# The first feed-forward product of a two-layer hybrid backbone, computed per weight tile from seven half-sized products

## The chip, the core and the metric

The kernel runs on one core of one Trainium2 chip. Its engines are TensorE (PE, with PEld for the loads of its stationary operand), VectorE (DVE), ScalarE (ACT), GpSimd (POOL) and SyncE (SP); SP issues most transfers, POOL and ACT a few. The metric is the time of one execution on the device in microseconds; the median of three runs of the kernel before is 3309.47 us (3304.61 to 3312.08).

## What is computed

A generator's backbone of two layers runs over 1024 latent tokens and 256 context tokens of width 1024. Each layer normalises and modulates, mixes tokens with three groups of heads, and ends with a gated feed-forward stage (SwiGLU) of inner width 2816. The last layer drops the context after its keys and values.

```python
def swiglu(h, w_in, w_out):
    gate, up = jnp.split(h @ w_in, 2, axis=-1)
    return (jax.nn.silu(gate) * up) @ w_out

def hybrid_layer(xl, xc, sc, scc, ...):
    mod_l = sc @ w_mod + b_mod
    sh1, sc1, gt1, sh2, sc2, gt2 = [m[:, None, :] for m in jnp.split(mod_l, 6, axis=-1)]
    ...
    h2 = modulate(rms_norm(xl, g_ffn), sh2, sc2)
    xl = xl + gt2 * swiglu(h2, w_ffn_in, w_ffn_out)
```

(The last two lines are the reference's feed-forward stage in short.) The context goes through the same stage in layer one with modulations of its own.

## The kernel before, in words

Activations lie with channels on the 128 partitions and tokens along the free dimension, in eight tiles k of 128 channels. The latent tokens are two halves b of 512; the context is one group of 256. Every operand of a large product is split in two (`split`, L126 to L129): ACT rounds it to fp32r (L128), DVE subtracts to get the remainder (L129). A product is then three matmuls, high by high, low by high and high by low (`mm3`, L144 to L146). `weight` (L130 on) loads a weight tile on SP's queue (L135) into one of two buffers `wr` and splits it into `wh` and `wl`, two buffers each.

The feed-forward stage is `ffn` (L1051). It goes through 22 inner tiles f in blocks of 3, 3, 3, 3, 3, 3, 2, 2. For each f it loads the gate's and the up's weight tile (1024 columns wide after the split, eight k of 128) and computes for each token group 24 matmuls for the gate and 24 for the up into the two halves of one PSUM tile `ps_f`. ACT takes the Silu of the gate (L1074), DVE multiplies by the up (L1075), and the result is split into `gh` and `gl`, which stay in SBUF. At a block's end the second product adds the block's tiles to the residual stream: per output tile m, three matmuls per f and group into `ps_fo`, and DVE adds them to x (`residual`, L1002). The groups in layer one are half 0, context, half 1; in layer two there is no context. In the last block the groups are taken one after the other, each with its first and second product, and after each the next norm (layer one) or the final norm and the output (layer two) is done.

Ahead of the stage, `out_proj` computes half 1's last attention projection (L1194) while half 0 is normalised (L1190), and half 1 is normalised after it (L1196). The pages of this stage live in a pool that `phase` (L72) opens after the release of the attention's pool; x is loaded into it from DRAM (L1188). During layer one's stage, POOL computes the modulation sums of layer two (`mods_part`, L270 to L285): per 512 columns and k it loads 128 rows of `w_mod`, multiplies by the conditioning value of the row (L281) and adds (L283); `mods_sum` (L287) folds the sums on DVE.

No order is written out by hand. Each engine, SP's queue included, runs its instructions in a fixed order. The framework has set that order ahead of the run: an instruction is placed when its operands and its buffer are expected to be free, and among those that are free at once the one that stands earlier in the program goes first. PSUM has four kinds of buffers: two tiles `ps_s` of two banks, two tiles `ps_t`, one `ps_g` and one `ps_o`.

Of the kernel before, what the change touches and what calls it, by code (L numbers as in the profile page):

```python
# [9 lines left out]
F32 = mybir.dt.float32  # L10
# [5 lines left out]
T = 1024  # L16
# [37 lines left out]
class Net:  # L54
# [16 lines left out]

    def tl(self, shape=(128, 512), name="tl"):  # L72
        return self.pool.tile(list(shape), F32, tag="tl", name=name, bufs=4)
# [67 lines left out]
    def mm3(self, ps, w, x, first, last):  # L141
        (wh, wl), (xh, xl) = w, x
        mm = self.nc.tensor.matmul
        mm(ps, wh, xh, start=first, stop=False)  # L144
        mm(ps, wh, xl, start=False, stop=False)  # L145
        mm(ps, wl, xh, start=False, stop=last)  # L146


    def setup(self):
# [36 lines left out]
        self.tabd = [tc.dram_tile([4, 128, 896], F32, name=f"tabd{l}") for l in range(2)]  # L186
        self.yc_c = tc.dram_tile([128, 4, TC], F32, name="yc_c")
# [82 lines left out]
    def mods_part(self, l, c, pages):  # L270


        nc, G = self.nc, self.nc.gpsimd
        nj = 2 if l == 0 or c < 4 else 1
        acc = pages[:2]
        for k in range(KD):
            w, o = pages[2 + k % 2], pages[3 - k % 2]
            G.dma_start(w, self.a["w_mod"][l, k * 128:(k + 1) * 128, c * 512:(c + 1) * 512])
            for j in range(nj):
                to = acc[j] if k == 0 else o if j < nj - 1 else w  # L280
                G.tensor_tensor(to, w, self.sc[:, k, j:j + 1].to_broadcast([128, 512]), op=ALU.mult)  # L281
                if k > 0:
                    G.tensor_tensor(acc[j], acc[j], to, op=ALU.add)  # L283
        for j in range(nj):
            G.dma_start(self.modd[l][j, :, c * 512:(c + 1) * 512], acc[j])  # L285
# [765 lines left out]
    def ffn(self, l, groups, blocks, parts, done, aside=None, keep=False):  # L1051
# [4 lines left out]
        for bi, nf in enumerate(blocks):  # L1056
# [4 lines left out]

            for gi in [[i for i, _ in p] for p in parts] if last else [range(len(groups))]:
                gs = []
                for f in range(f0, f0 + nf):
                    wg, wu = self.wk(a["w_ffn_in"][l, f]), self.wk(a["w_ffn_in"][l, KF + f])
                    row = {}
                    for i in gi:
                        h, xs, n, j, place = groups[i]
                        gh, gl = place(f - f0)
                        ps = self.ps_s("ps_f")  # L1070
                        for p, w in enumerate((wg, wu)):
                            self.proj(ps[:, p * 512:p * 512 + n], w, h)
                        sg = self.hp(name="sg")[:, :n]
                        nc.scalar.activation(sg, ps[:, :n], AF.Silu)  # L1074
                        nc.vector.tensor_tensor(sg, sg, ps[:, 512:512 + n], op=ALU.mult)  # L1075
                        self.split(gh, gl, sg)
                        row[i] = (gh, gl)
                    gs.append(row)
                    if aside and gi[0] == 0:
                        aside(f)  # L1080
                pieces = dict(x for p in parts for x in p)
                for gj, c in [((i,), c) for i in gi for c in pieces[i]] if last else [(gi, None)]:
                    for m in range(KD):
# [6 lines left out]
                        for i in gj:  # L1090
                            h, xs, n, j, place = groups[i]
                            s = c or slice(0, n)
                            ps = self.ps_gt("ps_fo")[:, :s.stop - s.start]
                            for k in range(nf):
                                gh, gl = gs[k][i]
                                self.mm3(ps, (w[0][:, k], w[1][:, k]), (gh[:, s], gl[:, s]), k == 0, k == nf - 1)
                            self.residual(xs[m][:, s], ps, self.ls[l]["mod"][:, 40 + m, j:j + 1])
                    if last:
                        done(gj[0], c)
            f0 += nf  # L1100


    def run(self):
        nc, a, tc = self.nc, self.a, self.tc
        with ExitStack() as es:
# [29 lines left out]
            for l in range(2):  # L1135
# [50 lines left out]
                for b in range(2):  # L1186
                    for k in range(KD):
                        nc.sync.dma_start(xg[b][k], xd[:, k, tb[b]])  # L1188
                h2 = [(self.big("h2h"), self.big("h2l"))]
                self.norm(xg[0], 512, l, 1, 0, *h2[0], self.nw, self.ps_t)  # L1190
                if full:
                    h2c = (self.bigc("h2ch"), self.bigc("h2cl"))
                    self.norm(XC, TC, 0, 1, 1, *h2c, self.nw, self.ps_t)
                self.out_proj(l, 0, [(mix[1], xg[1], 512, 0, None, None)], self.ps_h, engine=nc.gpsimd)  # L1194
                h2.append((self.big("h2h"), self.big("h2l")))
                self.norm(xg[1], 512, l, 1, 0, *h2[1], self.nw, self.ps_t)  # L1196

                def place(b):
                    def p(f):
                        if b == 0:  # L1200
                            place.cur[f] = (self.pg(dt=F32R, name="gh"), self.pg(dt=F32R, name="gl"))
                        return tuple(t[:, tb[b]] for t in place.cur[f])
                    return p

                place.cur = {}
                turn = count()

                def placec(f):
                    t = self.pool.tile([128, 2, TC], F32R, tag="nw", name="gc", bufs=self.nnw)
                    return t[:, 0], t[:, 1]  # L1210
# [146 lines left out]
```

## Time and profile before

| | |
|---|---|
| median of three runs | 3309.47 us |
| the profiled execution, its time | 3303.53 us |
| the profiled execution, its span | 3301.7 us |
| TensorE busy | 3176.8 us, 96% |
| VectorE busy | 1704.9 us, 52% |
| ScalarE busy | 979.0 us, 30% |
| GpSimd busy | 542.2 us, 16% |
| layer one's feed-forward stage | about 880 to 1812 us |
| layer two's feed-forward stage | about 2549 us to the end |

Span means from the first to the last instruction. Views by stretch say how much of a stretch each engine was busy, with the clock that TensorE was granted as a share of full speed. The views by line group equal instructions; the timelines list single instructions with their start and duration, in brackets the idle time ahead of them and what ended it.

### The profile page before, as it was taken

How to read it: one execution, taken by the hardware profiler on the slowest of the kernel's cores; microseconds unless marked ns; L12 is line 12 of the kernel's file. 1: busy time of each engine (PE TensorE's matmuls, PEld its weight loads, DVE VectorE, ACT ScalarE, POOL GpSimd, SP SyncE). 2: the span in 40 equal slices, each digit the busy share in tenths (PEclk: the TensorE clock that was granted, in tenths of full speed). 3: DMA queues.
4: the chain of work that ended last, by engine and by line, in shares of the span. 5: the costliest groups of instructions: out<-in, count | busy, mean ns of one | idle time of the engine just before them, and what ended most of it. 6: DMA issues, size and time to landing. Idle time of an engine off the chain costs nothing. (4 is left out here: it accounts for less than half of the span.)

```text
span 3301.7 us, 41939 instructions
## 1 busy us (share of the span) xinstructions
PE 3176.8 (96%) x16750; PEld 2502.6 (76%) x16750; DVE 1704.9 (52%) x2781; ACT 979.0 (30%) x1724; POOL 542.2 (16%) x525
## 2 busy tenths in 40 slices
PE   5999999999899999999999999999998999999998
PEld 2677776666688888888887887776666788888886
DVE  7865846555633433323446985944656423333235
ACT  4323335433521111111114432334434211111113
POOL 2011310000177788400000100400001000000001
PEclk9999999998999999999999999999899999999999
DMA  5656741345322334201113337631445011111122
GB/s 207 210 174 193 234 156 49 100 149 168 124 72 91 110 110 129 91 28 60 61 48 125 114 93 242 200 112 53 149 151 168 30 48 55 53 46 54 35 64 77
DMA packets 209271, 365.96 MB, mean 111 GB/s; under 512 B 18754, under 2 KB 112628, under 8 KB 206772
## 3 DMA queue, kind: packets, MB, share of 16 engines
q1 hardware_dynamic: 145600, 267.93, 25.2%
q0 software_dynamic: 13840, 58.73, 5.7%
q10 hardware_dynamic: 49636, 36.62, 3.5%
q8 instruction: 132, 2.16, 0.3%
q14 instruction: 63, 0.52, 0.0%
HBM read 284.39 MB, written 78.82 MB: 110 GB/s over the span
## 5 line engine op out<-in xcount | busy, mean ns | idle before, releaser
L144 PE MATMUL ps_f<-h2h,wh 128*128 128x512 f32 x1408 | 550.8, 391 | 8.1 <-ACT h2h L343 3.5
L145 PE MATMUL ps_f<-h2l,wh 128*128 128x512 f32 x1408 | 551.3, 392 | 2.2 <-DVE h2l L344 1.2
L146 PE MATMUL ps_f<-h2h,wl 128*128 128x512 f32 x1408 | 551.0, 391 | 0.3 <-DVE wl L129 0.3
L128 ACT CAST wh<-wr 128x1024 fp32r<-128x1024 f32 (+2 forms) x306 | 239.2, 782 | 925.4 <-PE ps_fo L145 415.1
L129 DVE TENSOR_TENSOR wl<-wr,wh 128x1024 fp32r<-128x1024 f32 (+2 forms) x288 | 284.0, 987 | 402.4 <-ACT wh L128 398.5
L144 PEld LDWEIGHTS ps_f<-h2h,wh 128*128 128x128 f32 x1408 | 265.5, 189 | 65.3 <-ACT wh L128 5.6
L145 PEld LDWEIGHTS ps_f<-h2l,wh 128*128 128x128 f32 x1408 | 265.4, 188 | 58.9 <-DVE h2l L129 2.1
L146 PEld LDWEIGHTS ps_f<-h2h,wl 128*128 128x128 f32 x1408 | 265.4, 188 | 56.8 <-issue 1.0
L1002 DVE SCALAR_TENSOR_TENSOR x<-ps_fo,mod,x 128x512 f32<-128x512 f32 (+1 forms) x264 | 192.2, 733 | 205.2 <-PE ps_fo L146 204.7
L144 PE MATMUL ps_in<-hh,wh 128*128 128x512 f32 x704 | 284.1, 404 | 4.3 <-ACT qkv L523 1.8
L146 PE MATMUL ps_in<-hh,wl 128*128 128x512 f32 x704 | 280.8, 399 | 0.0
L145 PE MATMUL ps_in<-hl,wh 128*128 128x512 f32 x704 | 280.4, 399 | 0.0
L1075 DVE TENSOR_TENSOR sg<-sg,ps_f 128x512 f32<-128x512 f32 (+1 forms) x110 | 69.5, 632 | 391.5 <-ACT sg L1074 391.5
L145 PE MATMUL ps_fo<-gl,wh 128*128 128x512 f32 x672 | 262.9, 391 | 0.0
L144 PE MATMUL ps_fo<-gh,wh 128*128 128x512 f32 x672 | 262.1, 391 | 0.0
L146 PE MATMUL ps_fo<-gh,wl 128*128 128x512 f32 x672 | 261.1, 390 | 0.0
L1074 ACT ACTIVATE sg<-ps_f 128x512 f32<-128x512 f32 (+1 forms) x110 | 60.8, 552 | 403.2 <-PE ps_f L146 403.2
L144 PEld LDWEIGHTS ps_in<-hh,wh 128*128 128x128 f32 x704 | 133.4, 190 | 45.0 <-issue 8.0
L146 PEld LDWEIGHTS ps_in<-hh,wl 128*128 128x128 f32 x704 | 133.2, 189 | 32.4 <-issue 5.3
L145 PEld LDWEIGHTS ps_in<-hl,wh 128*128 128x128 f32 x704 | 133.6, 190 | 30.0 <-issue 5.2
L283 POOL TENSOR_TENSOR pm<-pm,pm 128x512 f32<-128x512 f32 x112 | 154.6, 1380 | 7.2
L638 PE MATMUL ps_S<-qkv,qkv 64*128 64x128 f32 (+2 forms) x544 | 144.8, 386 | 4.2 <-DMA qkv<-qkv 2.3
(317 smaller groups left out, 5722.6 us busy)
## 6 DMA issues: line engine op xcount, KB each, us to landing
wr<-in_w_ffn_in SPq DMA_DIRECT2D x96, 512.0 KB
pm<-in_w_mod POOLq DMA_DIRECT2D x96, 256.0 KB, 3.2
wr<-in_w_in SPq DMA_DIRECT2D x44, 512.0 KB
wr<-in_w_ffn_out SPq DMA_DIRECT2D x96, 192.0 KB
wmod<-in_w_mod POOLq DMA_DIRECT2D x16, 1024.0 KB, 5.4
qkv<-qkv SPq DMA_DIRECT2D x32, 512.0 KB
wr<-in_w_out SPq DMA_DIRECT2D x48, 256.0 KB
x_dram<-xo SPq DMA_DIRECT2D x48, 256.0 KB
```

Source lines behind the costliest of these rows:

```text
L128: self.nc.scalar.copy(hi, src)
L129: (engine or self.nc.vector).tensor_tensor(lo, src, self.f(hi), op=ALU.subtract)
L144: mm(ps, wh, xh, start=first, stop=False)
L145: mm(ps, wh, xl, start=False, stop=False)
L146: mm(ps, wl, xh, start=False, stop=last)
L283: G.tensor_tensor(acc[j], acc[j], to, op=ALU.add)
L638: nc.tensor.matmul(S[:, c0:c1], heads[h], kap, start=True, stop=True)
L1002: self.nc.vector.scalar_tensor_tensor(xap, ps, gate, xap, op0=ALU.mult, op1=ALU.add)
L1074: nc.scalar.activation(sg, ps[:, :n], AF.Silu)
L1075: nc.vector.tensor_tensor(sg, sg, ps[:, 512:512 + n], op=ALU.mult)
```

## The change

Let the weights of one f be four quarters: A11 and A12 the gate's channels k 0 to 3 and 4 to 7, A21 and A22 the same of the up. Let the activations be four quarters: B11 and B21 half 0's channels 0 to 3 and 4 to 7, B12 and B22 half 1's. Gate and up of both halves are then a product of 2 by 2 blocks, and the change computes it with seven block products and sums (the form named after Strassen and Winograd), of 12 matmuls of 512 columns each. The sums of weights S1 to S4 are made for every f on DVE and split like the weights; the sums of activations T1 to T4 are made once per layer (`blocks`). Partial results stay in PSUM and three are copied out by ACT. This holds for f = 0 to 17 in layer one and 0 to 16 in layer two. The last four or five f are computed whole as before, but in two steps: half 0 ahead of the seven-product tiles, half 1 behind them. The context's 48 matmuls of 256 columns come at the end of each f.

The feed-forward stage is cut in two pools. In the first all 22 f of the first product are computed and the gated tiles written to DRAM; in the second they are loaded back, split, and the second product runs block by block (`ffn_out`). The modulation sums of layer two are computed by DVE with fused multiply-adds instead of by POOL, which still issues their loads; their folding moves into the second pool's blocks. In the last block the groups have only their second products.

```diff
-    def mods_part(self, l, c, pages):
+    def mods_part(self, l, c):
+        acc = [self.ev(name="macc") for _ in range(2 if c < 4 else 1)]
         for k in range(KD):
-            G.dma_start(w, self.a["w_mod"][l, k * 128:(k + 1) * 128, c * 512:(c + 1) * 512])
...
+            w = self.tp(name="wmodp")
+            nc.gpsimd.dma_start(w, self.a["w_mod"][l, k * 128:(k + 1) * 128, c * 512:(c + 1) * 512])
+            for j, o in enumerate(acc):
+                v = self.sc[:, k, j:j + 1]
+                if k == 0:
+                    V.tensor_scalar(o, w, v, None, op0=ALU.mult)
+                else:
+                    V.scalar_tensor_tensor(o, w, v, o, op0=ALU.mult, op1=ALU.add)
...
+    def blocks(self, l, b1, raw, X):
+        rs = self.rstd(X, 512, self.ev, self.ps_t)
+        for k in range(4):
+            x1, x2, b11, b21 = X[k], X[4 + k], raw[k], raw[4 + k]
+            self.norm_of(k, x1, rs, l)
+            self.norm_of(4 + k, x2, rs, l)
+            self.nc.sync.dma_start(self.b12d[l][:, k], x1)
+            V.tensor_tensor(b11, x1, b11, op=ALU.subtract)
+            self.split(t1[0][:, k], t1[1][:, k], b11)
+            e = self.ev(name="t2")
+            V.tensor_tensor(e, x2, b11, op=ALU.subtract)
+            self.split(t2[0][:, k], t2[1][:, k], e)
+            V.tensor_tensor(b21, b21, e, op=ALU.subtract)
+            self.split(hi[:, k], lo[:, k], x2)
+            V.tensor_tensor(b11, x2, x1, op=ALU.subtract)
+            self.split(hi[:, 4 + k], lo[:, 4 + k], b21)
+        t3 = [self.st(f"t3{p}") for p in "hl"]
+        for k in range(4):
+            self.split(t3[0][:, k], t3[1][:, k], raw[k])
...
+    def prod(self, ps, w, x, first, last):
+        for k in range(4):
+            c = slice(k * 128, (k + 1) * 128)
+            self.mm3(ps, (w[0][:, c], w[1][:, c]), (x[0][:, k], x[1][:, k]), first and k == 0, last and k == 3, True)
+
+    def hidden7(self, l, f, B, hc):
+        for i in range(2):
+            r = m.tile([128, 1024], F32, tag="wr", name="wr", bufs=2)
+            nc.sync.dma_start(r, self.a["w_ffn_in"][l, f + i * KF])
+            wh = m.tile([128, 1024], F32R, tag="wh", name="wh", bufs=2)
+            wl = m.tile([128, 1024], F32R, tag="wl", name="wl", bufs=2)
+            self.split(wh, wl, r)
...
+        V.tensor_tensor(s1, a21, a22, op=ALU.add)
+        self.split(*S1, s1)
+        V.tensor_tensor(s2, s1, a11, op=ALU.subtract)
+        self.split(*S2, s2)
+        V.tensor_tensor(a21, a11, a21, op=ALU.subtract)
+        self.split(*S3, a21)
+        V.tensor_tensor(a12, a12, s2, op=ALU.subtract)
+        self.split(*S4, a12)
...
+        p1, p2, p5 = self.ps_t(name="ps_p"), self.ps_go(name="ps_q"), self.ps_h(name="ps_r")
+        self.prod(p1, half(0, 0), B["11"], True, False)
+        nc.scalar.copy(u1, p1)
+        self.prod(p5, S1, B["t1"], True, False)
+        nc.scalar.copy(u5, p5)
+        self.prod(p1, S2, B["t2"], False, False)
+        nc.scalar.copy(u2, p1)
+        self.prod(p2, half(0, 512), B["21"], True, True)
+        V.tensor_tensor(u1, u1, p2, op=ALU.add)
+        nc.scalar.activation(u1, u1, AF.Silu)
+        self.prod(p1, S3, B["t3"], False, False)
+        V.tensor_tensor(u5, u5, p1, op=ALU.add)
+        self.prod(p5, S4, B["22"], False, True)
+        V.tensor_tensor(u2, u2, p5, op=ALU.add)
+        nc.scalar.activation(u2, u2, AF.Silu)
+        V.tensor_tensor(u2, u2, u5, op=ALU.mult)
+        nc.sync.dma_start(g[:, 512:], u2)
+        self.prod(p1, half(1, 512), B["t4"], False, True)
+        V.tensor_tensor(u1, u1, p1, op=ALU.mult)
+        nc.sync.dma_start(g[:, :512], u1)
+        if hc:
+            pc = self.ps_h(name="ps_f")
+            for i in range(2):
+                self.proj(pc[:, i * TC:(i + 1) * TC], [x.rearrange("p (k c) -> p k c", k=KD) for x in w[i]], hc)
+            self.gated(pc[:, :TC], pc[:, TC:], self.gdc[f])
...
-    def ffn(self, l, groups, blocks, parts, done, aside=None, keep=False):
+    def ffn_out(self, l, groups, blocks, parts, done, aside=None, keep=False):
+            for f in range(nf):
+                r = self.pg(name="graw")
+                nc.sync.dma_start(r, self.gd[l][f0 + f])
+                for t in (slice(0, 512), slice(512, T)) if last else [slice(0, T)]:
+                    self.split(gh[:, f, t], gl[:, f, t], r[:, t])
...
-                self.phase(f"ffn{l}", 15, 3, nnw=4, nfx=1)
+                self.phase(f"ffna{l}", 0, 0)
+                xh = [self.st("x2", F32), self.st("x2", F32)]
+                for i in range(2):
+                    nc.sync.dma_start(xh[i], xd[:, 4 * i:4 * i + 4, tb[1]])
+                b1, raw = self.first_half(l, xd)
...
+                self.out_proj(l, 0, [(mix[1], xs, 512, 0, None, xd[:, :, tb[1]])], self.ps_h, engine=nc.gpsimd)
+                two = range(KF - (4 if full else 5), KF)
+                for f in two:
+                    w = self.w_in(l, f)
+                    self.hidden(w, [(*b1, ks)], self.gd[l][f, :, :512])
+                    if full:
+                        self.hidden(w, [(*h2c, ks)], self.gdc[f])
+                B = self.blocks(l, b1, raw, xs)
+                for f in range(two[0]):
+                    self.hidden7(l, f, B, h2c)
+                    if full:
+                        for c in range(12):
+                            if f == 1 + 4 * c // 3:
+                                self.mods_part(1, c)
...
+                for f in two:
+                    self.hidden(self.w_in(l, f), [(*b12, ks[:4]), (*B["22"], ks[4:])], self.gd[l][f, :, 512:])
+
+                self.phase(f"ffnb{l}", 14, 3, nnw=8, nfx=1)
                 X = [self.pg(name=f"x{k}") for k in range(KD)]
+                for k in range(KD):
+                    nc.sync.dma_start(X[k], xd[:, k, :])
```

`first_half` loads half 0 in eight pages and normalises and splits it; `norm_of` is one multiply on DVE and one scaled copy on ACT; `hidden` computes one whole tile of one group as before; `gated` takes Silu and product and writes the tile to DRAM. `tp` and `ev` are pages of 512 columns, eight buffers each, `st` pages of four times that, six buffers.

## Rows read from the trace of the kernel before

**Rows 1.** The page: span, busy time of each engine (share of the span), instructions

```profile
span 3301.7 us, 41939 instructions
PE 3176.8 (96%) x16750; PEld 2502.6 (76%) x16750; DVE 1704.9 (52%) x2781; ACT 979.0 (30%) x1724; POOL 542.2 (16%) x525
```

**Rows 2.** Busy us of each engine by stretch (instruction counts); granted clock, DMA share, GB/s

```profile
1000.00:1100.00 100.00, 100.00 (x523) 86.20 (x522) 31.69 (x36) 16.19 (x26) 76.46 (x75) 1.00 0.29 89
2700.00:2800.00 100.00, 100.00 (x442) 82.56 (x442) 31.25 (x43) 18.59 (x28) 0.00 (x0) 1.00 0.15 48
```

**Rows 3.** Timeline of TensorE, two context matmuls: start, duration, line, tiles, shapes

```profile
1055.72 0.28 PE L144 MATMUL ps_f<-h2ch,wh 128*128 128x256 f32 x1
1055.84 0.28 PE L145 MATMUL ps_f<-h2cl,wh 128*128 128x256 f32 x1
```

**Rows 4.** Instruction groups by line and shape: count, busy us, mean ns, idle before

```profile
L128 ACT CAST wh<-wr 128x1024 fp32r<-128x1024 f32 x140 | 147.1, 1051 | 406.0 <-PE ps_f L145 237.4 <-PE ps_fo L145 114.1 <-PE ps_in L145 35.1
L1002 DVE SCALAR_TENSOR_TENSOR x<-ps_fo,mod,x 128x512 f32<-128x512 f32 x248 | 185.2, 750 | 203.1 <-PE ps_fo L146 202.8
L128 ACT CAST gh<-sg 128x512 fp32r<-128x512 f32 x88 | 54.6, 620 | 87.3 <-DVE sg L1075 87.3
L1075 DVE TENSOR_TENSOR sg<-sg,ps_f 128x512 f32<-128x512 f32 x88 | 60.3, 685 | 333.8 <-ACT sg L1074 333.8
L281 POOL TENSOR_TENSOR pm<-pm,scc 128x512 f32<-128x512 f32 x128 | 139.0, 1087 | 59.3 <-DMA pm<-in_w_mod 48.2 <-DMA modd<-pm 9.6
L316 DVE RECIPROCAL rs<-rs 128x512 f32<-128x512 f32 x9 | 30.2, 3352 | 14.3 <-ACT rs L315 14.3
```

**Rows 5.** Timeline of VectorE: one remainder of a weight tile in each layer

```profile
1073.49 2.74 DVE L129 TENSOR_TENSOR wl<-wr,wh 128x1024 fp32r<-128x1024 f32 x1 [3.80 <-ACT wh L128]
2598.29 1.23 DVE L129 TENSOR_TENSOR wl<-wr,wh 128x1024 fp32r<-128x1024 f32 x1 [3.65 <-ACT wh L128]
```

**Rows 6.** What TensorE waited for, 895 to 920 us: total, times, longest

```profile
PE ps_f L144 <- ACT h2h L343: 3.5, 1, 3.5
```

**Rows 7.** Stretches of rows 2's view around TensorE's pauses for the second half's norm

```profile
900.00:910.00 10.00, 5.52 (x24) 3.85 (x23) 9.78 (x12) 6.54 (x10) 0.00 (x0) 0.82 0.01 2
910.00:920.00 10.00, 10.00 (x39) 8.10 (x38) 5.76 (x9) 4.63 (x7) 2.99 (x8) 0.84 0.28 79
2570.00:2580.00 10.00, 9.24 (x32) 6.92 (x33) 4.36 (x6) 3.51 (x6) 0.00 (x0) 0.83 0.14 51
```

**Rows 8.** Timeline of SP's transfers at layer one's change of pool

```profile
813.50 0.40 SPq L1021 DMA_DIRECT2D x_dram<-xo  x1
...
841.30 0.32 SPq L1021 DMA_DIRECT2D x_dram<-xo  x1
844.27 8.99 SPq L1188 DMA_DIRECT2D x<-x_dram  x16
```

**Rows 9.** The same at layer two's change of pool

```profile
2513.19 0.32 SPq L1021 DMA_DIRECT2D x_dram<-xo  x1
...
2514.58 10.22 SPq L1188 DMA_DIRECT2D x<-x_dram  x16
```

**Rows 10.** Stretches of rows 2's view in which those loads ran

```profile
850.00:860.00 10.00, 8.96 (x29) 5.17 (x30) 7.19 (x7) 5.94 (x9) 1.12 (x1) 1.00 0.92 331
2520.00:2530.00 10.00, 7.43 (x22) 3.91 (x23) 6.47 (x7) 6.78 (x11) 1.27 (x1) 1.00 1.01 357
```

**Rows 11.** Timeline of ScalarE: the first instruction on a loaded page

```profile
847.34 0.63 ACT L325 ACTIVATE sq<-x 128x512 f32<-128x512 f32 x1 [2.21 <-DMA x<-x_dram]
```

**Rows 12.** Timeline of VectorE at the end of layer one: norm of the first half

```profile
1761.39 3.35 DVE L316 RECIPROCAL rs<-rs 128x512 f32<-128x512 f32 x1 [0.78 <-ACT rs L315]
...
1776.84 0.69 DVE L129 TENSOR_TENSOR hl<-xr,hh 128x512 fp32r<-128x512 f32 x1
```

**Rows 13.** Timeline of VectorE at the kernel's end

```profile
3284.65 2.09 DVE L1002 SCALAR_TENSOR_TENSOR x<-ps_fo,mod,x 128x256 f32<-128x256 f32 x5
...
3293.00 3.64 DVE L1227 SCALAR_TENSOR_TENSOR o<-x,small,rs 128x256 f32<-128x256 f32 x4
```

More of the change, by code (lines that the diff above doesn't have):

```diff
@@ new lines, in gated, with hidden @@
+    def gated(self, gate, up, dst):
+        n = dst.shape[-1]
+        g = self.ev(name="g")[:, :n]
+        self.nc.scalar.activation(g, gate, AF.Silu)
+        self.nc.vector.tensor_tensor(g, g, up, op=ALU.mult)
+        self.nc.sync.dma_start(dst, g)
+    def hidden(self, w, h, dst):
+        ps = self.ps_s("ps_f")
+        n = dst.shape[-1]
+        for p in range(2):
+            o = ps[:, p * 512:p * 512 + n]
+            for i, (hh, hl, ks) in enumerate(h):
+                for k in range(len(ks)):
+                    self.mm3(o, (w[p][0][:, ks[k]], w[p][1][:, ks[k]]), (hh[:, k], hl[:, k]),
+                             i + k == 0, i == len(h) - 1 and k == len(ks) - 1)
+        self.gated(ps[:, :n], ps[:, 512:512 + n], dst)
@@ L1060, in ffn @@
                 kept = self.keep(a["w_ffn_out"][l, :, :, f0:f0 + nf, :], nf)
-            for gi in [[i for i, _ in p] for p in parts] if last else [range(len(groups))]:
[L1063 to L1080, printed above, removed]
+            gh, gl = (self.big(n).rearrange("p k t -> p (k t)").rearrange("p (f t) -> p f t", t=T) for n in ("gh", "gl"))
+            gs = [{} for _ in range(nf)]
+            for f in range(nf):
[3 more added lines that the diff above has]
+                    self.split(gh[:, f, t], gl[:, f, t], r[:, t])
+                for b in range(2):
+                    gs[f][b] = gh[:, f, b * 512:(b + 1) * 512], gl[:, f, b * 512:(b + 1) * 512]
+                if len(groups) > 2:
+                    t = self.pool.tile([128, 2, TC], F32R, tag="nw", name="gc", bufs=self.nnw)
+                    r = self.hp((128, TC), name="grawc")
+                    nc.sync.dma_start(r, self.gdc[f0 + f])
+                    self.split(t[:, 0], t[:, 1], r)
+                    gs[f][2] = t[:, 0], t[:, 1]
+            for gi in [[i for i, _ in p] for p in parts] if last else [range(len(groups))]:
                 pieces = dict(x for p in parts for x in p)
@@ new lines, in run @@
+                B = self.blocks(l, b1, raw, xs)
+                for f in range(two[0]):
+                    self.hidden7(l, f, B, h2c)
+                    if full:
+                        for c in range(12):
+                            if f == 1 + 4 * c // 3:
+                                self.mods_part(1, c)
+                b12 = self.st("b12h"), self.st("b12l")
+                for k in range(4):
+                    t = self.tp(name="b12")
+                    nc.sync.dma_start(t, self.b12d[l][:, k])
+                    self.split(b12[0][:, k], b12[1][:, k], t)
@@ L1190, in run @@
-                self.norm(xg[0], 512, l, 1, 0, *h2[0], self.nw, self.ps_t)
-                if full:
[L1192 to L1210, printed above, removed]
+                for k in range(KD):
+                    nc.sync.dma_start(X[k], xd[:, k, :])
+                if full:
+                    XC = self.load_ctx(self.xc_dram, nc.gpsimd)
                 def final(b, c):
```

113 lines of the change are left out of this document (74 added, 39 removed).

## The prediction, made before the changed kernel ran

> **What bounds the kernel now.** I read the page first: TensorE is busy for 96% of the span, no other engine for more than 52% [rows 1]. A busy TensorE is not yet a full one, so the view by stretch comes next. In both feed-forward stages TensorE is busy without a gap at full clock, 442 matmuls in 100 us in layer two: a pitch of 0.2262 us for 512 columns [rows 2]. The context's 256 columns have a pitch of 0.12 us [rows 3]. One inner tile f of layer one is 96 of the first and 48 of the second, 21.7 + 5.8 = 27.5 us. Here time goes only if matmuls go, and it comes back only where TensorE waits. Last come the pauses around the stages, since the change moves their borders: the norm of half 1 (rows 6 and 7), the change of pool (rows 8 to 11), the end of layer one (rows 12) and of the kernel (rows 13).
>
> **The seven products.** 7 x 12 = 84 matmuls stand for 96, in 18 + 17 = 35 tiles: 420 fewer, 420 x 0.2262 = **-95.0 us**. All of it was on the path [rows 2].
>
> What they add beside TensorE, per tile: on DVE two remainders of 1024 columns at 1.23 us (the value with POOL silent [rows 5]), four sums, four remainders and five combinations of 512 columns at 0.69 [rows 4], 2.5 + 9.0 = 11.4 us. On ACT two casts at 1.05 and four casts, three copies and two Silus at about 0.62 [rows 4], 7.7 us. A tile lasts 84 x 0.2262 = 19.0 us in layer two and 24.8 with the context in layer one, so both have room. Layer two's sums come on top in layer one: 4 chunks x 16 + 8 x 8 = 128 multiply-adds at 0.75 (the nearest row, the residual's [rows 4]), 96 us in 18 x 24.8 = 446 us; in the four tiles with 16 of them DVE has 11.4 + 12 + 0.4 of 24.8 us. POOL's arithmetic cost nothing to the path before and is worth nothing now.
>
> So the question is latency, not load. Each product covers 12 x 0.2262 = 2.7 us. A PSUM copy or combination (0.6 to 0.75 us) that must be over before the next accumulation into `p1` has one product of cover. The sums of the next tile need only its raw weights; both raw buffers come free when S3 and S4 are split, some 5 us into a tile, and two loads of 0.52 MB at 331 GB/s take about 3.2 us [rows 10]. S1 and S2 can thus be ready 5 us or more ahead of their tile. The gate's split buffer comes free with the fourth product, with the context only 24 x 0.12 = 2.9 us ahead of the tile's end, against a chain of 1.05 + 1.23. The up's comes free at the very end, but its first reader is the seventh product and S3 the fifth. No stall, then, if the queues are ordered so. Bounds 0 and 0.7 us per tile (one DVE instruction in the way); I take 0.25: **+9 us**.
>
> **Half 1's norm** now runs under four or five whole tiles (10.9 us each, 16.6 with the context). Before, TensorE idled for 4.5 us in layer one, 3.5 of them for ScalarE's h2h [rows 6], and 0.8 in layer two, and the granted clock read 0.82, 0.84 and 0.83 [rows 7]. Time at the low level of 1.2 GHz is twice what is missing from the mean: 6.8 us, 4.5 of them idle, and 3.4 with 0.8 idle. The rest lost half its work, 1.2 + 1.3 us. **-8 us**. What takes its place: T1 to T4 and half 1's split need 4 x 11 = 44 DVE instructions, 30 us, 26% of DVE goes to the whole tiles' weights, and the norm ahead of them takes about 8 us (eight squares at 0.62 on ACT, the reciprocal's 3.35 [rows 4]): 8 + 30/0.74 = 49 of layer two's 54 us. Bounds 0 and 6, I take **+2 us**.
>
> **The start of the first pool.** Half 1 (2.1 MB) now stands ahead of half 0's pages in SP's queue; at 331 to 357 GB/s [rows 10] that is 6 us of delay for half 0's norm, with `out_proj` as part cover. Bounds 0 and 6 per layer, I take 3: **+6 us**.
>
> **The second pool** is where most of the gain may go back. Its first matmul needs a gated tile from DRAM, and nothing is left for TensorE by then. The trace shows a change of pool with loads behind it twice. x's first row lay in DRAM from 813.5 us on, yet all sixteen loads of x follow the last store of the old pool, 841.3 to 844.3 [rows 8] and 2513.2 to 2514.6 [rows 9]. If that holds here, then from the last matmul: Silu and product 1.4 us, store 0.4, then eight loads of x of 0.52 MB stand ahead of the first tile in program order; nine times 0.52 MB at 331 to 357 GB/s are 13.2 to 14.3 us, plus about 1 us of landing beyond that, and a cast of 1.05 [rows 4]. Sum 18. Below it, if the tile went first, 1.4 + 0.4 + 3.1 (issue at 844.27 to use at 847.34 [rows 8, 11]) + 1.05 = 6 us; nothing at all if the loads ran ahead of the old pool's end; above it 24, with the context's pages ahead too. I take 18, since both rows of this kind agree, and 1.3 us of half clock behind the pause as in rows 7: 2 x 19.3 = **+39 us**.
>
> The Trainium skill says in TensorE: Matmul & The Clock Gate (section "Why this matters for your kernels") that an idle gap between bursts sends TensorE back to half rate; the clock in rows 7 agrees, and these two new gaps are where the rule speaks against the change. By it the price is still the 1.3 us each.
>
> Writing and reading back 11.5 MB per layer each way hides: DMA is 15 to 30% busy there [rows 2]. The second product's matmuls are the same.
>
> **The end of layer one.** Half 0's norm took 16.1 us from the start of the reciprocal to the last remainder (1761.39 to 1777.5 [rows 12]), with eight squares at 0.62 ahead of it about 21 us, under half 1's first product. Now only half 1's second product (10.9 us) and the context's (5.8) lie over it, and DVE owes half 1's residuals and norm behind it. Half 0's norm ends some 10 us after half 1's products could, and half 1's norm starts that much later, with 5.8 us of the context as cover; I take **+6 us** (0 to 15). **The kernel's end**: the last residual began at 3284.65 and the output's multiply ran to 3296.6 [rows 13]. Half 0's final norm (3.35 + 8 x 0.69 = 8.9 us of DVE) used to lie under 21.7 us of first products; now it competes with half 1's residuals in 11.6 us: **+4 us** (0 to 8).
>
> **The sum:** -95 + 9 - 8 + 2 + 6 + 39 + 6 + 4 = -37 us. The profiled execution took 3303.5 us, so 3266.5; the median of the runs is 5.9 us above it: **3272 us**.
>
> **Rivals.** *Loads ahead of time.* If the second pool's loads run while the whole tiles of half 1 are computed, its 39 us shrink to 6 or less, and the time is 3272 - 33 = 3239 us. For it: the pools reuse memory tile by tile. Against it: rows 8 and 9.
>
> *Slower: the up's remainder ahead of the sums.* If in ACT's and DVE's queues the split of the up's weights stands ahead of S1, every tile starts, after the up's buffer is released at the tile border, with 1.05 + 1.23 + 0.69 + 0.62 + 0.69 us [rows 4, 5] and some 0.4 us of handing over: 4.7 us against 2.7 of cover, a stall of 2 us in each of 35 tiles, 70 us in place of 9: 3333 us. It decides from (37 + 9)/35 = 1.3 us per tile. For it: the program has that order. Against it: S1 is ready sooner.
>
> *Late loads of `w_mod`.* POOL waited 48 us in total for these loads before [rows 4]. DVE waits in their place now, with evictions behind it; if all that reaches TensorE, 3272 + 48 = 3320 us, the gain gone; a third of it is likelier. The Trainium skill's SBUF — State Buffer (section "Who interferes with whom") has it that two-input DVE instructions collide with POOL's reads, and DVE's two-port forms with any POOL access; rows 5 agree, 2.74 against 1.23 us. By that rule POOL's issue work could wait for DVE now, which no run here shows.
>
> **Chances.** Forecast 0.50 (3255 to 3300), loads ahead 0.23, up's split first 0.14, late loads 0.13. The likeliest gives 3272; the range from 3232 (loads ahead, no stalls at the ends) to 3318 (late loads) leaves out most of the third and a little below. A difference under 0.2%, about 6.6 us, can't be told from none here. Faster: 0.50 + 0.23 + 0.02 = 0.75; the same 0.10; slower 0.15.
>
> **What would show it.** Seven-product stretches with 442 matmuls per 100 us in layer two; a pause of TensorE of 15 to 20 us ahead of each first `ps_fo`, with SP's loads of x starting behind the last store; no repeated wait for S1 or the up's remainder. Wrong would be a pause under 8 us there, or one recurring per tile above 0.7 us.

## The result and the profile after

The changed kernel took 3398.95 us (3393.82 to 3404.99) where the kernel before took 3307.26 us beside it: a ratio of 1.0276, with a 95% interval of 1.0254 to 1.0298. It is 92 us slower; the forecast was 3272 us, faster. The page of the profiled execution, its span, engines and granted clock by slices (tenths), answers to [rows 1]:

```profile
span 3395.5 us, 42438 instructions
PE 3108.9 (92%) x16330; PEld 2433.7 (72%) x16330; DVE 2029.4 (60%) x3328; ACT 1144.0 (34%) x1985; POOL 241.2 (7%) x282
PEclk9999999999889999998999899999999989998999
```

TensorE is busy for 68 us less and takes 94 us longer. What it waited for is in the view of waits (the instruction that waited, what released it; total, times, longest). First layer one's feed-forward stage, then layer two's:

```profile
PE ps_r L153 <- ACT s L137: 61.9, 5, 28.2
PE ps_fo L153 <- ACT hh L137: 19.0, 2, 9.5
PE ps_fo L153 <- ACT gh L137: 18.5, 1, 18.5
...
PE ps_r L153 <- ACT s L137: 28.2, 1, 28.2
PE ps_fo L153 <- ACT gh L137: 18.5, 1, 18.5
PE ps_fo L153 <- DVE x L1014: 5.9, 2, 4.7
```

The stretches of the seven products themselves are as forecast in layer two, without a gap at full clock (443 matmuls in 100 us, as in [rows 2]). In layer one's first ones they are not. Columns as in [rows 2]:

```profile
1000.00:1100.00 100.00, 80.11 (x396) 67.06 (x396) 57.99 (x89) 30.47 (x48) 9.71 (x18) 0.88 0.29 99
1100.00:1200.00 100.00, 79.44 (x396) 66.76 (x396) 57.43 (x87) 23.32 (x36) 10.77 (x20) 0.91 0.30 104
2800.00:2900.00 100.00, 100.00 (x443) 82.81 (x442) 56.97 (x80) 37.52 (x57) 0.00 (x0) 1.00 0.23 82
```

To see where the time went I cut both traces at the same instructions of TensorE and split each stage in three: the traced matmuls times their pitch (0.2262 us for 512 columns, 0.12 for 256, others by their columns), TensorE's idle time (the length less the busy time in the view by stretch), and what is left: time at half clock, the small matmuls' overhead, and waits too short to show between matmuls whose records overlap.

| stage, up to | before | after | change | matmuls | idle | left |
|---|---|---|---|---|---|---|
| mixer one, first `ps_out` | 627.7 | 643.1 | +15.4 | 0 | +5.0 | +10.4 |
| output projection, first `ps_f` | 248.6 | 255.7 | +7.1 | +1.0 | +6.6 | -0.5 |
| feed-forward one, first `ps_in` of layer two | 939.6 | 1019.0 | **+79.4** | -49.1 | +101.8 | +26.7 |
| mixer two, last `ps_o` | 674.8 | 654.8 | -20.0 | -0.7 | -4.1 | -15.2 |
| feed-forward two, end | 811.1 | 822.8 | **+11.7** | -46.1 | +52.3 | +5.5 |

The two mixers, which the change doesn't touch, nearly cancel. The matmuls fell by 95.2 us in the two feed-forward stages (420 fewer on the page): that step was right. Idle time took 154 us and the part left over 32. Four places hold most of the idle time.

**28.2 us, once in each layer**, ahead of the first seven-product tile. VectorE's timeline (start, duration):

```profile
979.62 3.35 DVE L328 RECIPROCAL rs<-rs 128x512 f32<-128x512 f32 x1 [2.03 <-ACT rs L327]
983.01 1.90 DVE L1067 TENSOR_TENSOR x<-x,rs 128x512 f32<-128x512 f32 x3
984.82 0.69 DVE L1095 TENSOR_TENSOR x<-x,x 128x512 f32<-128x512 f32 x1
...
1006.48 0.70 DVE L138 TENSOR_TENSOR b2l<-x,b2h 128x512 fp32r<-128x512 f32 x1
1007.08 0.70 DVE L1155 TENSOR_TENSOR s<-wr 128x512 f32<-128x512 f32 x1
```

Half 1's whole norm and T1 to T4 run here, back to back, and S1 (L1155) behind them. The last matmul of half 1's output projection began at 904.8 us and 66 us of whole tiles followed, but the squares, too, start only at 972.6 us on ACT, behind the last whole tile's gating (ScalarE's timeline), as the program has it:

```profile
972.32 0.38 ACT L1113 ACTIVATE g<-ps_f 128x256 f32<-128x256 f32 x1
972.60 0.62 ACT L337 ACTIVATE sq<-x 128x512 f32<-128x512 f32 x1
```

Half 1's last residual ended at 906.1 us on DVE, and ACT then stood idle for 8 to 10 us in each of the four whole tiles. Why the framework didn't move the squares up into that time (their pages are shared with the gated tiles) no run here shows; the runs below show what their place costs.

**8.4 us, four times**, in layer one's tiles behind a modulation chunk with two outputs:

```profile
1055.78 0.48 DVE L293 TENSOR_SCALAR macc<-wmodp,scc 128x512 f32<-128x512 f32 x1
1057.80 0.42 DVE L1114 TENSOR_TENSOR g<-g,ps_r 128x256 f32<-128x256 f32 x1 [1.54 <-ACT g L1113]
1058.14 0.48 DVE L293 TENSOR_SCALAR macc<-wmodp,scc 128x512 f32<-128x512 f32 x1
1058.53 9.36 DVE L295 SCALAR_TENSOR_TENSOR macc<-wmodp,scc,macc 128x512 f32<-128x512 f32 x14
1067.81 1.22 DVE L138 TENSOR_TENSOR wl<-wr,wh 128x1024 fp32r<-128x1024 f32 x1
1068.94 0.68 DVE L1155 TENSOR_TENSOR s<-wr 128x512 f32<-128x512 f32 x1
```

Fourteen multiply-adds stand in one piece ahead of the up's remainder and S1.

**18.5 us, once in each layer**, at the change of pool, as forecast (SP's timeline, to be read beside [rows 8, 9]):

```profile
1558.42 0.33 SPq L1115 DMA_DIRECT2D gd<-g  x1
1558.80 4.26 SPq L1366 DMA_DIRECT2D x<-x_dram  x8
1564.00 0.32 SPq L1209 DMA_DIRECT2D graw<-gd  x1
```

**9.5 us, twice** at the end of layer one: both `ps_fo` waits stand where a norm lies ahead of the residuals that free PSUM (in [rows 12] the first of these norms lay under half 1's first products). VectorE's timeline for the first, with 9.5 us of the norm between two residuals:

```profile
1874.98 0.65 DVE L1014 SCALAR_TENSOR_TENSOR x<-ps_fo,mod,x 128x512 f32<-128x512 f32 x1
1875.55 0.74 DVE L354 SCALAR_TENSOR_TENSOR xr<-x,ab,rs 128x512 f32<-128x512 f32 x1
...
1885.05 1.41 DVE L1014 SCALAR_TENSOR_TENSOR x<-ps_fo,mod,x 128x512 f32<-128x512 f32 x2
```

### The profile page after: what moved, and what is told of

The parts are those of the page before. It is cut to its first block, busy times and chain, and to the rows that moved or that the text cites. A ratio compares the mean times of both kernels' runs of the same rounds, so it can differ in the third digit from the quotient of the medians.

```text
span 3395.5 us, 42438 instructions
## 1 busy us (share of the span) xinstructions
PE 3108.9 (92%) x16330; PEld 2433.7 (72%) x16330; DVE 2029.4 (60%) x3328; ACT 1144.0 (34%) x1985; POOL 241.2 (7%) x282
## 5 line engine op out<-in xcount | busy, mean ns | idle before, releaser
L137 ACT CAST wh<-wr 128x1024 fp32r<-128x1024 f32 (+2 forms) x316 | 249.8, 791 | 780.0 <-PE ps_fo L154 363.9
L153 PEld LDWEIGHTS ps_fo<-gh,wh 128*128 128x128 f32 x672 | 128.1, 191 | 73.7 <-ACT gh L137 37.8
L657 ACT ACTIVATE P<-P,ast 128x640 f32<-128x640 f32 (+4 forms) x144 | 121.3, 843 | 91.3 <-DVE ast L654 80.1
L155 PEld LDWEIGHTS ps_fo<-gh,wl 128*128 128x128 f32 x672 | 128.1, 191 | 27.7 <-DVE wl L138 0.4
L154 PEld LDWEIGHTS ps_fo<-gl,wh 128*128 128x128 f32 x672 | 128.1, 191 | 26.2 <-DVE gl L138 1.5
L153 PE MATMUL ps_r<-t0h,s 128*128 128x512 f32 x140 | 61.4, 439 | 90.8 <-ACT s L137 90.1
L677 PE MATMUL ps_P<-co,P 128*128 128x128 f32 (+1 forms) x752 | 123.2, 291 | 6.1 <-DVE P L665 5.9
L677 PEld LDWEIGHTS ps_P<-co,P 128*128 128x128 f32 (+1 forms) x752 | 83.0, 143 | 56.5 <-issue 43.9
L153 PE MATMUL ps_out<-mh,wh 128*128 128x512 f32 x256 | 109.6, 428 | 15.1 <-DVE x L1014 8.4
L388 DVE SCALAR_TENSOR_TENSOR cout<-craw,small,cout 128x1021 f32<-128x1021 f32 (+2 forms) x96 | 122.8, 1280 | 0.7
```

Of the source, the lines that this page charges most:

```text
L137: self.nc.scalar.copy(hi, src)
L153: mm(ps, wh, xh, start=first, stop=False, skip_group_check=skip)
L154: mm(ps, wh, xl, start=False, stop=False, skip_group_check=skip)
L155: mm(ps, wl, xh, start=False, stop=last, skip_group_check=skip)
L388: nc.vector.scalar_tensor_tensor(out[:, s:e], raw[:, s + d:e + d], w[:, ct * 7 + j:ct * 7 + j + 1], out[:, s:e], op0=ALU.mult, op1=ALU.add)
L657: nc.scalar.activation(p, p, AF.Exp, scale=-1.0, bias=nm[:, h:h + 1], accum_out=su[:, h:h + 1])
```

## The experiments

All runs are read against the kernel before, which ran beside them: the ratios compare runs, the medians less well. "One" and "two" are the lengths of the feed-forward stages of the table above, in the one traced execution of each run.

| run | median us | ratio (95% interval) | one | two |
|---|---|---|---|---|
| the change | 3399.0 | 1.0276 (1.0254 to 1.0298) | 1019.0 | 822.8 |
| T1 to T4 ahead of whole tiles | 3386.1 | 1.0210 (1.0159 to 1.0260) | 1006.8 | 816.4 |
| T1 to T4 in parts between them | 3343.7 | 1.0101 (1.0072 to 1.0130) | 989.5 | 792.6 |
| chunks in halves | 3369.6 | 1.0158 (1.0109 to 1.0208) | 978.2 | 823.0 |
| gated tiles loaded first | 3392.9 | 1.0232 (1.0172 to 1.0293) | 1011.9 | 810.9 |
| norms late | 3389.0 | 1.0235 (1.0203 to 1.0268) | 1005.3 | 823.8 |
| last block of four | 3399.9 | 1.0269 (1.0246 to 1.0292) | 1017.0 | 820.6 |
| sums first | 3391.8 | 1.0236 (1.0201 to 1.0270) | 1006.5 | 822.9 |
| four edits | 3290.3 | 0.9939 (0.9919 to 0.9959) | 935.4 | 782.2 |
| four edits, eight products | 3351.1 | 1.0128 (1.0101 to 1.0154) | 966.9 | 827.7 |
| sums first and even chunks | 3273.7 | 0.9875 (0.9846 to 0.9903) | 920.0 | 782.3 |
| the same, fewer whole tiles | 3264.5 | 0.9853 (0.9824 to 0.9882) | 914.4 | 777.1 |
| the same, norms late | 3254.0 | 0.9822 (0.9790 to 0.9854) | 902.9 | 775.8 |

**T1 to T4 ahead of the whole tiles, in one piece.**

```diff
+                    if f == two[0]:
+                        B = self.blocks(l, b1, raw, xs)
                     w = self.w_in(l, f)
...
-                B = self.blocks(l, b1, raw, xs)
```

> The changed kernel (3399 us) with one edit: half 1's norm and its 40 DVE instructions for T1 to T4 are issued ahead of the whole tiles of half 0 and not behind them. Theory (DVE's queue is served in order, and this run of about 35 us of work stalls TensorE wherever it stands in one piece): the two pauses of 28.2 us ahead of the first seven-product tiles go, and some 20 us of them come back as a wait of the whole tiles for their gating, since two PSUM pages hold only one tile of layer one: 3375 to 3395 us. Rival (only the place was wrong, five whole tiles give cover enough): both pauses go without replacement, 3399 - 56 = 3343 us or a little less.

Measured: 3386 us. The 28.2 us are gone; in their place (TensorE's waits, layer one, then two)

```profile
PE ps_f L153 <- DVE g L1114: 15.0, 2, 12.3
...
PE ps_f L155 <- DVE wl L138: 22.3, 1, 22.3
```

15.0 us for the gating of a whole tile and 22.3 for a weight's remainder, both queued behind the piece. So moving the piece to another place, still in one piece, is not enough.

**The same work in parts between the whole tiles.** `blocks` is a generator here, advanced once ahead of the loop.

```diff
+                part = self.blocks(l, b1, raw, xs)
+                next(part)
                 for f in two:
...
+                    for _ in range(((1, 2, 2, 0) if full else (1, 1, 1, 2, 0))[f - two[0]]):
+                        B = next(part)
```

> The changed kernel with one edit: half 1's norm is issued ahead of the whole tiles of half 0, and the T1 to T4 work in four parts between them (one, two and two behind the first three tiles in layer one; one, one, one and two behind the first four in layer two). Theory (queue order on DVE): the two pauses of 28.2 us ahead of ps_r fall to under 3 us each, and no new pause takes their place; 3399 - 50 to 60 = 3340 to 3349 us. Rival (there is too much DVE work for the whole tiles to hide): a pause of at least 10 us remains in each layer, 3375 us or more.

Measured: 3343.7 us, as the theory had it. From the first whole tile to the second seven-product tile of layer one the view of waits has one row, for the first tile's weights:

```profile
PE ps_f L153 <- ACT wh L137: 3.3, 1, 3.3
```

In layer two 0.5 us is the longest wait of `ps_f` and no `ps_r` waits. The whole tiles do hide norm and T1 to T4, as long as the pieces between two gatings are short.

**The modulation's chunks in halves.**

```diff
...
-                            if f == 1 + 4 * c // 3:
-                                self.mods_part(1, c)
+                        if 1 <= f < 9:
+                            self.mods_part(1, (f - 1) // 2, range(4) if f % 2 else range(4, KD))
+                        elif 9 <= f < 17:
+                            self.mods_part(1, f - 5)
```

> The changed kernel with one edit: the four modulation chunks with 16 multiply-adds are given out in two halves of 8 to two tiles each; loads and sums stay the same in number. Theory (16 multiply-adds stand in one piece of 10.6 us ahead of S1 in DVE's queue): the four waits of 8.4 us for S1 go, with 5 to 10 us of half clock behind them, 3354 to 3368 us. Rival (DVE waits for the loads of w_mod): the same loads, so the waits only move, 3390 to 3400 us. Rival (the up's remainder ahead of S1): as many waits as before, 3390 to 3400 us.

Measured: 3369.6 us, 1.6 us above the expected range. The four waits are gone, with the same 96 loads; the framework now places a chunk's multiplies and multiply-adds as eight, three, three and two with the products' combinations between them. That the loads were late is also ruled out by the change's own trace (groups by shape on VectorE: total, mean ns, idle before), where the multiply-adds never waited:

```profile
L295 DVE SCALAR_TENSOR_TENSOR macc<-wmodp,scc,macc 128x512 f32<-128x512 f32 x112 | 79.3, 747 | 0.0
```

**S1 and S2 ahead of the weights' splits.**

```diff
-            self.split(wh, wl, r)
             raw.append(r)
...
         self.split(*S2, s2)
+        for (wh, wl), r in zip(w, raw):
+            self.split(wh, wl, r)
```

> The changed kernel (3399 us) with one edit: in each seven-product tile the sums and splits of S1 and S2 are issued ahead of the splits of the two weights. Rival of the record (the up's remainder ahead of S1 delays each tile): the four waits of 8.4 us fall under 2 us, and the waits of 0.5 us for S1 in the later tiles go: 3355 us or less. Theory (the chunk of 16 multiply-adds, which still stands ahead of S1, is what costs): the four waits shrink by the one remainder that they are moved past, 1.2 us each, to about 7.2 us: 3390 to 3397 us.

Measured: 3391.8 us. Less the first tile's 28.2, the row below leaves four waits of 7.2 to 7.3 us, the theory's number; but the 0.5 us waits of the eight later tiles also went, as the rival said. Stage one is 12.5 us shorter, of which 4.6 are the four waits; the rest lies in the eight later tiles, some 1.1 us shorter each.

```profile
PE ps_r L153 <- ACT s L137: 57.3, 5, 28.2
```

**Gated tiles ahead of x in SP's queue.**

```diff
-                for k in range(KD):
-                    nc.sync.dma_start(X[k], xd[:, k, :])
+                def load():
+                    for k in range(KD):
+                        nc.sync.dma_start(X[k], xd[:, k, :])
...
+            if bi == 0:
+                load()
```

> The changed kernel with one edit: in the second pool the eight loads of x are issued behind those of the first three gated tiles. Theory (the pause of 18.5 us ahead of the first ps_fo is SP's queue: eight loads of 0.52 MB stand ahead of the gated tile): the pause falls to 6 to 8 us in each layer, 3373 to 3380 us. Rival (the pool's memory or the last store holds the loads back): it stays above 15 us, 3395 us or more.

The pauses fell to 7.8 us in both layers, as expected; the median fell by less than expected: the ratio by 0.44%, some 15 us, which its interval doesn't tell from the 19.0 us (7.1 + 11.9) by which the two stages got shorter. SP's timeline, where a gated tile now follows the last store at 1562.73 us:

```profile
1562.73 0.33 SPq L1115 DMA_DIRECT2D gd<-g  x1
1563.11 0.42 SPq L1209 DMA_DIRECT2D graw<-gd  x1
```

and TensorE's first second product:

```profile
1568.99 1.22 PE L153 MATMUL ps_fo<-gh,wh 128*128 128x512 f32 x2 [7.82 <-ACT gh L137]
```

**The end of layer one, twice.** Once each norm is issued a group later (`owed` holds one call of `done` back):

```diff
-                        done(gj[0], c)
+                        owed.append((gj[0], c))
+                        if not keep and len(owed) > 1:
+                            done(*owed.pop(0))
...
```

> The changed kernel (3399 us) with one edit: at the end of layer one each norm is issued one group later (half 0's behind half 1's residuals, half 1's behind the context's). Theory (each norm is a run of 11 us of DVE work in one piece ahead of the next group's residuals, so the second products wait for PSUM pages): the two waits of 9.5 us inside the second products go; but half 0's norm then ends some 10 us after the last second product, so TensorE waits there ahead of layer two's first projection instead: 3385 to 3400 us. Rival (DVE has gaps enough for the norms): 3370 to 3378 us and no wait over 4 us ahead of the projection.

Once the last block has four hidden tiles:

```diff
-                blocks = (3, 3, 3, 3, 3, 3, 2, 2)
+                blocks = (3,) * 6 + ((4,) if full else (2, 2))
```

> The changed kernel with one edit: layer one's last block of the second product has four hidden tiles and not two, so that half 1's products there last 21.7 us and not 10.9, and the context's 11.5 and not 5.8. Theory (the end of layer one lacks TensorE work over the norms): the wait of 9.5 us for half 0's norm goes or falls under 2 us, that for half 1's ahead of the context's products shrinks by about the added 5.8 us; 14 to 17 us less in all, and up to 5 of half clock: 3377 to 3385 us. Rival (a run of 11 us of DVE work takes all PSUM pages whatever the length of the products): both waits stay above 6 us, 3390 us or more.

TensorE's waits at the end of layer one, with late norms:

```profile
PE ps_fo L153 <- DVE xc L1014: 11.5, 2, 9.3
```

and with the block of four:

```profile
PE ps_fo L155 <- DVE wl L138: 13.6, 4, 7.2
```

Late norms brought 13.7 us in stage one, and the median lies in the theory's range, but only one of the two waits went: half 0's norm now stands ahead of the context's residuals, so 9.3 us of wait stand among the context's second products, and none ahead of the projection, where the theory had it. The block of four missed: 2 us, as its rival had the time, though not the cause. With four tiles each `m` needs a weight tile of its own, whose remainder now stands behind the norm: a wait for PSUM was exchanged for one for weights.

**Four edits together** (parts, halves, gated first, block of four).

> The changed kernel with four edits together: T1 to T4 in parts between the whole tiles, the modulation chunks of 16 multiply-adds in halves, the gated tiles loaded ahead of x, and a last block of four in layer one. Theory (these pauses are separate and in a row on TensorE's path): the gains add, 3399 - 55 - 30 - 21 - 16 = 3277 us, within 10 us, and faster than the kernel before (3307 to 3312). Rival (one pause hides another, or the half clock eats the gain): 3300 us or more.

Measured: 3290.3 us, faster than before by 0.6% and 3 us above the expected band. The single ratios' gains add up to 3.4% and the run gained 3.4%; my sum was off since two of its terms were (gated tiles first and the block of four).

**The same with eight products.** Plain products for both halves and all 22 tiles, through DRAM and two pools all the same:

```diff
-                for f in two:
...
+                for f in range(KF):
                     w = self.w_in(l, f)
                     self.hidden(w, [(*b1, ks)], self.gd[l][f, :, :512])
...
-                    self.hidden7(l, f, B, h2c)
...
+                    self.hidden(w, [(*b2, ks)], self.gd[l][f, :, 512:])
```

> The kernel of the four edits, but with the first product as before in eight half-sized products' worth of matmuls (96 per tile and both halves), without the sums, T1 to T4 and combinations; the hidden tiles still go to DRAM and come back in a second pool. Theory (the seven products give all of their 95 us, since their work beside TensorE is hidden once it is in the right order): 85 to 95 us more than the four edits, about 3365 us, so the detour over DRAM alone costs 50 to 60 us against the kernel before. Rival (the sums cost half of it back): less than 60 us more, under 3337 us.

60.8 us more than the four edits, between theory and rival; the two stages give 77.0, and in the traced executions the first mixer takes 18 of that back (see the last section). Layer two gives 45.5 of the 46.1 us that 17 tiles are worth; layer one gives 31.5 of 48.9. Of the 17 us missing, 14 are lost in eight tiles of 26.7 us in place of 24.9, where S1 still stands behind the up's remainder and two multiply-adds in the four edits:

```profile
1233.11 0.74 DVE L297 SCALAR_TENSOR_TENSOR macc<-wmodp,scc,macc 128x512 f32<-128x512 f32 x1
1233.78 1.22 DVE L138 TENSOR_TENSOR wl<-wr,wh 128x1024 fp32r<-128x1024 f32 x1
1234.91 0.74 DVE L297 SCALAR_TENSOR_TENSOR macc<-wmodp,scc,macc 128x512 f32<-128x512 f32 x1
1235.58 0.68 DVE L1159 TENSOR_TENSOR s<-wr 128x512 f32<-128x512 f32 x1
```

Against the kernel before, the two stages with eight products are 27.3 + 16.6 us longer. That is not the detour over DRAM alone: 7.8 + 8.4 of it are TensorE's waits at the change of pool, and some 15 of the first stage are waits at the end of layer one.

**Sums first and even chunks** on top of the four edits.

> The kernel of the four edits (3290 us), but with S1 and S2 ahead of the weights' splits and the modulation's multiply-adds spread evenly: four loads of w_mod per tile over 18 seven-product tiles and six over each of the last four whole tiles. In the four edits eight seven-product tiles of layer one last 26.7 us in place of 24.9, with S1 behind two or more multiply-adds and the up's remainder on DVE. Theory (queue order): these tiles come down to 24.9 us, 8 x 1.8 = 14 us less: 3276 us, within 5. Rival (the loads of w_mod come late): the tiles with eight loads were the slow ones, so about the same gain; then DVE's idle time would stand ahead of the multiply-adds in the trace and not at S1.

Measured: 3273.7 us, as the theory had it. The rival fell: already in the four edits the multiply-adds had waited 0.0 us for their loads. A stretch of layer one in the four edits:

```profile
1250.00:1350.00 100.00, 97.05 (x502) 79.82 (x501) 62.19 (x94) 29.62 (x46) 16.19 (x31) 1.00 0.40 142
```

and the same stretch in this run:

```profile
1250.00:1350.00 100.00, 100.00 (x533) 86.73 (x532) 55.59 (x81) 31.32 (x49) 9.67 (x18) 1.00 0.35 116
```

Against eight products the two stages are now 46.9 + 45.4 = 92 us shorter: nearly all of the 95. The comparison is fair to the eight products, though they have the uneven chunks: in layer one their TensorE waits once, for 2.0 us at 917 us, between the first tile and the change of pool.

**One whole tile fewer in each layer**, then **late norms in place of the block of four**.

```diff
-                two = range(KF - (4 if full else 5), KF)
+                two = range(KF - (3 if full else 4), KF)
```

> The same as the run with sums and chunks, and one whole tile fewer in each layer: three and four in place of four and five, so that 19 and 18 tiles have seven products. Two tiles by 12 matmuls by 0.2262 us are 5.4 us less, if three and four whole tiles still cover half 1's norm and T1 to T4: 3271 us. Rival (the cover is used up): a new pause of over 5 us ahead of the first seven-product tile in each layer, 3280 us or more.

> The run with fewer whole tiles (3264 us), but at the end of layer one the last block has two hidden tiles again and each norm is issued one group later, as in the run of the late norms. Theory (the norms in one piece on DVE cost at the end of layer one, and the larger last block only exchanged waits for PSUM pages for waits for the weights' remainder): the first feed-forward stage with the end of layer one gets 8 to 12 us shorter, as the run of the late norms was against that of the larger block: 3253 to 3258 us. Rival (with the other pauses gone the wait ahead of the context's products grows in its place): 3262 us or more.

Measured: 3264.5 us, with no new pause, and 3254.0 us. The first is 6.5 us below its number: the stages got 10.8 us shorter and not 5.4, since a wait of 3.3 us went too and 12 matmuls of the output projection (2.7 us) fell on the other side of layer two's cut. The second is as its theory had it, 11.5 us less in the first stage. The medians alone show neither step, since their ratios' intervals overlap. The last run is 1.8% faster than the kernel before. Its trace still has 7.7 us at each change of pool and 9.3 among the context's last products:

```profile
span 3255.0 us, 42410 instructions
PE 3090.8 (95%) x16306; PEld 2430.2 (75%) x16306; DVE 2046.3 (63%) x3346; ACT 1138.9 (35%) x1991; POOL 242.1 (7%) x282
```

## Why the prediction was wrong, step by step

The sum was -37 us and the profiled executions differ by +94. Of these 131 us, some 54 are half 1's norm with T1 to T4, 39 the waits for S1 in layer one, 13 the end of layer one and 19 the lower clock behind the pauses, each beyond what the sum had for it.

- **Seven products, -95.0 us: right.** -95.2 us of matmuls; TensorE kept nearly all of it once the queues were in order (92 us between the runs with even chunks and eight products).
- **Half 1's norm and T1 to T4, -8 + 2 us: the step that failed most.** The sum of DVE's work was right (49 of 54 us, and the run in parts shows that it fits), but I took it to run under the whole tiles because there was room. The overlap failed: the program issues it behind them, and ACT and DVE took it up there: 2 x 28.2 us. The pieces' length counts as well: in one piece ahead of the whole tiles it cost 15.0 + 22.3 us. In parts between them the waits were gone.
- **Per-tile stalls, +9 us (0 to 0.7 each): right in layer two (none), wrong in layer one.** I gave the sums 24.8 us in which 24 us of DVE work fit, and did not ask in which order. Sixteen multiply-adds in one piece cost 4 x 8.4 us; the chunks of eight (one output), with the up's remainder ahead of S1, cost 1.8 us in each of eight tiles. With the sums first and nothing else changed, such a tile lasted 25.5 to 25.6 us, so about 1.1 of the 1.8 us is the remainder's place. The rival "up's remainder ahead of the sums" thus held in part, below its own 2 us and in 8 of 35 tiles.
- **Late loads of `w_mod`: fell.** The multiply-adds waited 0.0 us. The page named beside it (the Trainium skill's SBUF — State Buffer, "Who interferes with whom") let one ask whether POOL's issue work would wait for DVE; POOL's issues of `wmodp` took 0.54 us each, against 0.57 for the same loads before, and I saw no sign of it. DVE's remainders took 1.22 us on average over both layers with POOL's arithmetic gone, as reckoned from [rows 5].
- **First pool, +6 us: too low.** The stretch from the mixer's end to the first `ps_f` grew by 7.1 us in layer one and by 6.4 in layer two (58.2 to 64.6), against 3 each; 1.0 and 2.7 of that are matmuls that changed sides, so some 10 us in all. The stretch varied from 255.5 to 271.3 us in layer one between the builds, and that half 1's loads ahead of half 0's are the cause was not tested.
- **Second pool, +39 us: mechanism and size right.** 18.5 us twice, the loads of x behind the last store; with the gated tiles first it is 7.8, near the lower bound of 6. The rival "loads ahead of time" fell with it.
- **End of layer one, +6 us (0 to 15): mechanism right, mis-sized.** Two waits of 9.5 us, 19 for 6; I counted half 0's norm but left half 1's, in front of the context's residuals, under cover.
- **Kernel's end, +4 us: right.** 6.4 us of TensorE's waits (4.7 the longest), where before had 2.2.
- **Half clock, 1.3 us behind a pause: too low.** In layer one the part left over grew by 26.7 us. Some 10.7 of it belong to the eight tiles of 26.7 us, where the clock was full: that is what the part lost from the four edits (34.3) to the even chunks (23.6). The other 16 us over the eight pauses of 8 us and more are 2.0 us each; in layer two 5.5 us over two pauses are 2.8 each. The stretches during the first pause, the 10 us behind it and the 10 us after those show it:

```profile
980.00:1009.00 29.00, 1.18 (x6) 0.61 (x4) 28.97 (x45) 17.65 (x30) 0.00 (x0) 0.56 0.10 36
1009.40:1019.40 10.00, 9.74 (x33) 7.28 (x34) 5.84 (x11) 4.94 (x7) 0.00 (x0) 0.76 0.32 105
1019.40:1029.40 10.00, 10.00 (x60) 8.90 (x59) 5.20 (x8) 2.60 (x4) 1.66 (x3) 1.00 0.41 132
```

The granted clock reads 0.56 in the pause, close to 1.2 of 2.4 GHz, averages 0.76 in the 10 us behind it, which is 2.4 us of full-speed time missing, and is full again after. Behind four other pauses it averaged 0.73 to 0.84 over 10 us, 1.6 to 2.7 us missing. The rule of the Trainium skill's TensorE: Matmul & The Clock Gate ("Why this matters for your kernels"), that an idle gap sends TensorE back to half rate, agrees with these rows; the price that I put on it did not.

## What to carry to other kernels

Load that fits under TensorE's work is not hidden until its place in the queue is known: for every step that is added, write down what stands directly ahead of it on its engine, and what is queued directly behind it. Here runs of 9 us and more in one piece on DVE stalled TensorE when a sum, a gating, a weight's remainder or a residual that it needed next was queued behind them. The same work in short pieces between the evictions cost nothing. An edit that saves matmuls can be worth nearly all of its savings and still lose, so price each new pause with the half clock behind it (some 2 us here), and count the pauses over all tiles that have one.

## What was not expected of the hardware

The waits repeat to a tenth of a microsecond from build to build: 28.2, 8.4, 9.5 us came back in every trace in which their cause stood. The mixer of layer one, which no edit touches, did not: 627.7 us before, 630.0 with eight products, 635.8 to 648.1 in the other builds. Between eight products and the four edits (630.0 and 648.1) 16 of the 18 us are in the part left over, with the same matmuls, and the granted clock of the stage was 0.99 and 0.97. That time at the lower clock is not a matter of the build alone: eleven executions of the kernel before, beside the last runs, ranged from 3296.2 to 3323.2 us with mean granted clocks from 0.988 to 0.979. One execution of each build was traced, so how much belongs to the build stays open, and what sets it too.
